# A two-layer hybrid block on one core: block sums and low parts by adding DMA, and three modulation sums moved

## The chip, the cores and the metric

The kernel runs on one core of a Trainium2 chip. The metric is the device time of one execution in microseconds, as the median of several runs.

## The reference, cut to what matters

A diffusion transformer of two layers works on 256 latent and 256 context tokens of width 1024, batch 1, in float32. Both streams are laid side by side, so that most products have 512 columns.

```python
for i in range(2):                       # layer 0: short convolution, layer 1: grouped attention
    mod  = silu(c)     @ mod_w[i] + mod_b[i]     # nine chunks of 1024 for the latent stream
    modc = silu(c_ctx) @ mod_w[i] + mod_b[i]     # the same for the context stream
    lat += 0.5 * mod[2] * swiglu(rms(lat) * g0 * (1 + mod[1]) + mod[0], w13[i, 0], w2[i, 0])
    cx  += 0.5 * modc[2] * swiglu(...same with modc...)
    h, hc = the two streams normed with chunks 3 and 4
    y, yc = conv(h), conv(hc)   or   attention(h, hc)
    lat += mod[5] * y           # and cx, while it is still read
    lat += 0.5 * mod[8] * swiglu(lat normed with chunks 6 and 7, w13[i, 1], w2[i, 1])
    # the same for cx in layer 0; in layer 1 the context ends with the attention

def swiglu(h, w13, w2):                  # 1024 -> 2 x 2816 -> 1024
    gate, up = split(h @ w13)
    return (silu(gate) * up) @ w2
```

## The kernel before, in words

**Arithmetic.** Every float32 matrix is split into a rounded high part and the rest, the low part, and a product is three matmuls: high by high, high by low, low by high (`mm3`, L136 to L138). `split` (L107, L108) makes the two parts: ScalarE copies the raw tile into the high part, VectorE subtracts it from the raw tile. `split_far` (L112 to L114) does without VectorE: ScalarE writes the high part and its negative, and a DMA issued by GpSimd reads the raw weights once more from memory and adds them onto the negative, which gives the low part.

**Weights.** `load_raw` (L103) brings up to 128 x 1024 float32 (512 KB) through SyncE's queue into a ring of eight buffers, `wr`. The high and low parts go into rings of four buffers, `wh` and `wl`, which TensorE frees when it has used them.

**First products.** The input products of the swiglus and of the convolution run over `Pair`s: two rows of output tiles of 128 at a time, with a seven-product scheme after Strassen and Winograd in place of eight, on blocks of 512 by 256. The scheme needs sums of weight blocks (S1 to S4) and of activation blocks (T1 to T4). A Pair loads two raw tiles r1 and r2 that hold its four weight blocks. For S1 GpSimd writes the negative of one block (L710), and an adding DMA of GpSimd puts another one onto it (L713). VectorE forms S2 in place (L732) and S3, S4 (L740); `keep` splits each pair of sums with one 1024-wide `split`. `head` computes the products with A11 and A12, `five` the one with S1, `six` those with S2 and S4, `seven` and `four` those with S3 and A22, which are taken one Pair later. A22's parts come from `split_far`. The first two input tiles of a stage go by plain products in `opening`, while the norm of the second stream is still being made; `opening` also sets up the first Pair, called head there.

**Second products.** The 22 rows of hidden tiles are taken in thirds of 8, 7 and 7. After each third `project` multiplies what there is by the matching part of w2, for eight output tiles m; `ws2` loads and splits the weights of one m, and `get` keeps three m ahead. The first three m run interleaved with the last Pair's `seven` and `four`. A tile that doesn't end the swiglu is scaled by the modulation gate on ScalarE (L564) and added to x by an adding DMA of GpSimd (L567). In the last third VectorE does it (L573), the sums of squares for the next norm are gathered (`square_add`, L262), and the last two tiles are taken one stream after the other, so that the norm of the first stream (`rms_sum`, `rms_all`, `Blocks.block`) can be made while TensorE works on the second.

**Modulation.** Each of the 128 rows that remain after the start (56 of layer 0, 72 of layer 1) is a job: a 512 KB load, and one VectorE sum per stream (`mod_unit`, L177, 1024 products each), 224 sums in all. `tick(n)` lets n of them run at its place in the program; `tick(ev)` follows the first five tiles of each second product, and some Pairs. `mod_ready` and `gate_of` run at once whatever is still missing of a chunk that is needed.

**Order.** The start is written out by hand. Behind it the scheduler of the framework orders each engine's instructions by their place in the program and by when it reckons them ready; `tc.issue_after(i)` keeps instructions of i's engine behind i.

Of the kernel before, what the change touches and what calls it, by code (L numbers as in the profile page):

```python
# [9 lines left out]
F32 = mybir.dt.float32  # L10
# [6 lines left out]
P = 128  # L17
# [31 lines left out]
def hybrid_kernel(ctx: ExitStack, tc: tile.TileContext, a: dict, out: bass.AP):  # L49
# [51 lines left out]
    def load_raw(src, n=1024):  # L101
        raw = wp.tile([P, 1024], F32, name=nm("wr"), tag="wr", bufs=8)
        nc.sync.dma_start(raw[:, :n], src)  # L103
        return raw
# [143 lines left out]
        return get  # L248


    accs = {}

    def square_add(k, c0, c1):

# [9 lines left out]
    def rms_sum(s):  # L264

        pq = psmall("ss")
        for i in range(2):
            c = s * S + i * P
            nc.tensor.matmul(
                pq[:, S + i : S + i + 1], accs["t"][:, c : c + P], ones[:, 0:1],  # L270
                start=True, stop=True,
            )
        rs = tp.tile([P, 2], F32, name=nm("rs"), tag="rs")
        nc.scalar.activation(
            out=rs, in_=pq[:, S : S + 2], func=AF.Sqrt, scale=1.0 / D, bias=eps_t
        )
        ri = tp.tile([P, 2], F32, name=nm("ri"), tag="ri")
        nc.vector.reciprocal(ri, rs)
        return pq, ri
# [93 lines left out]
    class Blocks:  # L373
# [33 lines left out]
        def sums(self, n):  # L407

            r = self.raw
            b11, b12, b21, b22 = r[0, 0], r[0, 1], r[1, 0], r[1, 1]  # L410
            tt = nc.vector.tensor_tensor

            def keep(key, src):
                hi, lo = self.t[key] = hot("th"), hot("tl")
                split(hi, lo, src)

            if n == 0:
                tt(out=b11, in0=b12, in1=b11, op=ALU.subtract)
                keep("T1", b11)
            elif n == 1:  # L420
                tt(out=b12, in0=b22, in1=b12, op=ALU.add)
                tt(out=b22, in0=b22, in1=b11, op=ALU.add)
                keep("T2", b22)
            else:
                tt(out=b21, in0=b21, in1=b22, op=ALU.subtract)
                keep("T3", b12)
                keep("T4", b21)

    class FirstBlocks(Blocks):
# [13 lines left out]
        def sums(self):  # L443
            r = self.raw
            tt = nc.vector.tensor_tensor
            for key in ("T1", "T2", "T3", "T4"):
                self.t[key] = hot("th"), hot("tl")

            def keep(key, q, src):
                hi, lo = self.t[key]  # L450
                c = slice(q * T2, q * T2 + T2)
                split(hi[:, c], lo[:, c], src)

            b = lambda hf, s, q: r[2 * hf + q, s]
            for q in range(2):
                tt(out=b(0, 0, q), in0=b(0, 1, q), in1=b(0, 0, q), op=ALU.subtract)
                keep("T1", q, b(0, 0, q))
            for q in range(2):
                tt(out=b(0, 1, q), in0=b(1, 1, q), in1=b(0, 1, q), op=ALU.add)
                tt(out=b(1, 1, q), in0=b(1, 1, q), in1=b(0, 0, q), op=ALU.add)  # L460
                keep("T2", q, b(1, 1, q))
            for q in range(2):
                tt(out=b(1, 0, q), in0=b(1, 0, q), in1=b(1, 1, q), op=ALU.subtract)
                keep("T3", q, b(0, 1, q))
            for q in range(2):
                keep("T4", q, b(1, 0, q))
# [122 lines left out]
    def project(ws, src, nk, gate, tail, tot, late, ev, between=()):  # L589

        def products(ps, w, ks, c0, c1, wide=True):
            ms = [src(k, c0, c1) for k in ks]
            if wide and len(ms[0]) == 3:
                return mm_wide(ps, [w(k) for k in ks], ms, ks[0] == 0, ks[-1] == nk - 1)
            for k, m in zip(ks, ms):  # L600
                mm3(ps[:, : c1 - c0], w(k), m[:2], k == 0, k == nk - 1)

        nf = 3 if between else 2
        ahead = {}

        def get(m):
            for i in range(m, min(m + 3, KT)):
                if i not in ahead:
                    ahead[i] = ws(i)
            return ahead[m]  # L610

        w2 = [get(m) for m in range(nf)]
        p2 = [psum("py") for _ in range(nf)]
        cut = nk - 2 if between else nk - 1
        for i in range(nf):
            products(p2[i], w2[i], range(cut), 0, tot)
            if i < len(between):
                between[i]()
        if between:
            for i in range(nf):  # L620
                products(p2[i], w2[i], (nk - 2,), 0, tot)
        for i in range(nf):
            products(p2[i], w2[i], (nk - 1,), 0, tot)
            finish(i, p2[i], 0, tot, gate, tail, len(src(0, 0, tot)) == 3)
            tick(ev)

        for m in range(nf, KT - late):
            if tail and tot == S and m == KT - 2:
                ready()
            w = get(m)  # L630
            ps = psum("py")
            wide = len(src(0, 0, tot)) == 3 and m < KT - 1
            products(ps, w, range(nk), 0, tot, wide)
            finish(m, ps, 0, tot, gate, tail, wide)
            if m < 5 - late:
                tick(ev)
            if late and tail and m == KT - late - 2:
                ready()
        if late:

            wl = [get(m) for m in (6, 7)]
            for s in range(2):
                for i in range(2):
                    ps = psum("py")
                    products(ps, wl[i], range(nk // 2), s * S, s * S + S)
                    flush(1)
                    products(ps, wl[i], range(nk // 2, nk), s * S, s * S + S)
                    finish(6 + i, ps, s * S, s * S + S, gate, tail)
# [48 lines left out]
    class Pair:  # L697
# [5 lines left out]

        def __init__(self, src, h):
            self.h, self.w, self.src = h, {}, src
            r2 = load_raw(src[:, 1024:2048])
            r1 = wp.tile([P, 1024], F32, name=nm("wr"), tag="wr", bufs=8)
            nc.sync.dma_start(r1[:, T2:], src[:, T2:1024])

            nc.gpsimd.tensor_scalar(  # L710
                out=r1[:, :T2], in0=r2[:, :T2], scalar1=-1.0, scalar2=None, op0=ALU.mult
            )
            nc.gpsimd.dma_start(out=r1[:, :T2], in_=src[:, :T2], accum_op=ALU.add)  # L713
            self.raw = [r1, r2]
            ts = half()
            for i, key in enumerate(("A11", "A12")):
                self.w[key] = [t[:, i * T2 : i * T2 + T2] for t in ts]
                split(*self.w[key], self.raw[i][:, T2:])

        def keep(self, keys, part):  # L720
            hi, lo = half()
# [4 lines left out]
        def sums(self, n):  # L726

            r1, r2 = self.raw
            s1, s2 = r1[:, :T2], r1[:, T2:]
            tt = nc.vector.tensor_tensor  # L730
            if n == 0:
                tt(out=s2, in0=s2, in1=s1, op=ALU.subtract)  # L732
                self.keep(("S1", "S2"), r1)
                return
            self.w["A22"] = [
                wp.tile([P, T2], F32R, name=nm(t), tag=t, bufs=2) for t in ("w4h", "w4l")
            ]
            split_far(*self.w["A22"], r2[:, :T2], self.src[:, 1024 : 1024 + T2])
            v = lambda t: t.rearrange("p (a c) -> p a c", a=2)
            tt(  # L740
                out=v(r2), in0=v(r2), in1=s2.unsqueeze(1).to_broadcast([P, 2, T2]),
                op=ALU.subtract,
            )
            self.keep(("S3", "S4"), r2)
# [44 lines left out]
    def opening(h, srcs, post):  # L789

        w = [load_w(srcs[0])]
        pp = [(psum("pg"), psum("pu")) for _ in range(2)]
        w13_mm(pp[0], w[0], h, range(KT), 0, S)
        flush(1)
        w.append(load_w(srcs[1]))
        at = w13_mm(pp[1], w[1], h, range(2), 0, S)
        with tc.issue_after(at):
            flush()
        with tc.issue_after(every[-1]):
            w13_mm(pp[1], w[1], h, range(2, KT), 0, S)  # L800
        h.sums(0)
        w13_mm(pp[0], w[0], h, range(KT), S, T2)
        post(pp[0], 0)
        head = srcs[2]()
        h.sums(1)
        head.sums(0)
        w13_mm(pp[1], w[1], h, range(KT), S, T2)
        post(pp[1], 1)
        head.head()
        head.sums(1)  # L810
        h.sums(2)
        return head

    def ffn(l, b, h, tot, gate, tail, gs=(), ev=(0, 0), z=None):
        gs = list(gs)
        i0 = 0
        for t, n in enumerate(THIRDS):
# [78 lines left out]
            def ws2(m):  # L896
# [1 line left out]
                o = (m % 2) * n * P  # L898
                raw = load_raw(src[:, o : o + n * P], n * P)
                hi, lo = half()  # L900
                split(hi[:, : n * P], lo[:, : n * P], raw[:, : n * P])
                return lambda k: (hi[:, k * P : k * P + P], lo[:, k * P : k * P + P])

            cur = gs
# [722 lines left out]
```

## Time and profile before

| | |
|---|---|
| median of 3 runs | 1545.36 us (1543.89 to 1546.64) |
| profiled execution | 1544.66 us |
| its span, first to last instruction | 1542.9 us |
| TensorE, matmuls | busy 1533.0 us, 99% |
| VectorE | busy 1296.8 us, 84% |
| ScalarE | busy 850.5 us, 55% |
| GpSimd | busy 299.3 us, 19% |
| moved by DMA | 278.80 MB, mean 181 GB/s |

The stages, by when TensorE starts on them in the trace: the first swiglu to 376 us (its second products from 110, 224 and 333), the convolution to 549 (its output product from 510), the second swiglu to 897, the third to 1245, then attention and, from 1353, the last swiglu on 256 columns. In the rows PE is TensorE's matmuls and PEld its weight loads, DVE is VectorE, ACT ScalarE, POOL GpSimd and SP SyncE; L with a number is a line of the kernel. A row of a timeline has start and length in us, engine, line, operation, the tile written and those read, and in brackets the engine's idle time before it with what ended it. A row of the groups has the count, the busy time in us, the mean in ns, and the idle time before.

### The profile page before, as it was taken

What the parts mean: (1) busy time and instruction counts of PE and PEld (TensorE: products, weight loads), DVE (VectorE), ACT (ScalarE), POOL (GpSimd) and SP (SyncE); (2) the same over time, 40 slices, a digit from 0 to 9 for tenths busy, and PEclk for the clock granted to TensorE, in tenths of its full rate; (3) what the DMA queues carried; (4) which work ended last, traced back from release to release, by engine and by line L of the source; (5) the groups of instructions that cost most, each with busy time, mean ns of one, the idle gap of its engine ahead of it and who ended that gap; (6) DMA issues with size and microseconds to landing.
All of it is one profiled execution on the core that took longest, in us unless ns stands there. A gap on an engine that the chain in (4) does not pass through costs nothing.

```text
span 1542.9 us, 27460 instructions
## 1 busy us (share of the span) xinstructions
PE 1533.0 (99%) x10652; PEld 1424.7 (92%) x10652; DVE 1296.8 (84%) x1974; ACT 850.5 (55%) x1476; POOL 299.3 (19%) x265
## 2 busy tenths in 40 slices
PE   9999999999999999999999999999999999999999
PEld 7898998999999899989899899989999899998888
DVE  5889788898999999978979889958968788997676
ACT  5744554646665376446456476446456456774553
POOL 0003313402231012042142102142052002300000
PEclk9999999999999999999999999999999999999999
DMA  9568768775366645686796635786697743476562
GB/s 367 211 191 236 159 185 227 172 196 142 75 144 183 197 104 143 216 209 147 213 210 150 212 74 126 222 186 145 209 222 177 257 156 113 147 246 220 170 195 75
DMA packets 97474, 278.80 MB, mean 181 GB/s; under 512 B 11456, under 2 KB 13120, under 8 KB 97344
## 3 DMA queue, kind: packets, MB, share of 16 engines
q1 hardware_dynamic: 69408, 228.10, 45.8%
q0 software_dynamic: 25920, 47.20, 18.1%
q10 hardware_dynamic: 2016, 1.76, 0.4%
q8 instruction: 83, 1.36, 0.4%
q14 instruction: 47, 0.39, 0.1%
HBM read 262.07 MB, written 1.05 MB: 171 GB/s over the span
## 4 chain that ended last, share of the span: by engine, by line
PE 90%; DVE 5%; DMA 2%; issue 1%; ACT 1%; POOL 0%; SPq 0%; DVEq 0%; ACTq 0%; POOLq 0%
PE py L137 8%; PE py L136 8%; PE py L138 8%; PE p L138 8%; PE p L136 8%; PE p L137 8%; PE q L138 6%; PE q L136 6%; PE q L137 6%; PE py L144 2%; PE pu L144 2%; PE pg L144 2%; DMA wr<-in_w 2%; DVE wl L108 1%; PE py L146 1%
## 5 line engine op out<-in xcount | busy, mean ns | idle before, releaser
L107 ACT ACTIVATE wh<-wr 128x1024 fp32r<-128x1024 f32 (+2 forms) x454 | 401.3, 909 | 291.0 <-PE py L137 98.6
L108 DVE TENSOR_TENSOR wl<-wr,wh 128x1024 fp32r<-128x1024 f32 (+2 forms) x454 | 467.0, 1052 | 106.3 <-ACT wh L107 87.6
L177 DVE CUSTOM_DVE_ANT_0 junk<-wr,scbc,first 128x1024 bf16<-128x1024 f32 x209 | 271.0, 1296 | 2.3 <-DMA wr<-in_modT 0.3
L137 PE MATMUL py<-gl,wh 128*128 128x512 f32 (+1 forms) x570 | 213.4, 374 | 0.0
L136 PE MATMUL py<-gh,wh 128*128 128x512 f32 (+1 forms) x570 | 213.4, 374 | 0.0
L138 PE MATMUL py<-gh,wl 128*128 128x512 f32 (+1 forms) x570 | 212.8, 373 | 0.0
L710 POOL TENSOR_SCALAR wr<-wr 128x512 f32<-128x512 f32 x66 | 123.5, 1871 | 423.8 <-DMA wr<-in_w 223.0
L136 PE MATMUL p<-th,wh 128*128 128x256 f32 x528 | 149.5, 283 | 0.1
L138 PE MATMUL p<-th,wl 128*128 128x256 f32 x528 | 149.4, 283 | 0.0
L137 PE MATMUL p<-tl,wh 128*128 128x256 f32 x528 | 149.4, 283 | 0.0
L138 PEld LDWEIGHTS py<-gh,wl 128*128 128x128 f32 x570 | 107.3, 188 | 19.2
L136 PEld LDWEIGHTS py<-gh,wh 128*128 128x128 f32 x570 | 107.4, 188 | 18.3
L137 PEld LDWEIGHTS py<-gl,wh 128*128 128x128 f32 x570 | 107.4, 188 | 18.1
L138 PE MATMUL q<-bh,wl 128*128 128x256 f32 x400 | 113.2, 283 | 0.0
L136 PE MATMUL q<-bh,wh 128*128 128x256 f32 x400 | 113.2, 283 | 0.0
L137 PE MATMUL q<-bl,wh 128*128 128x256 f32 x400 | 113.2, 283 | 0.0
L136 PEld LDWEIGHTS p<-th,wh 128*128 128x128 f32 x528 | 101.3, 192 | 0.7 <-ACT sg L757 0.3
L137 PEld LDWEIGHTS p<-tl,wh 128*128 128x128 f32 x528 | 101.3, 192 | 0.4
L138 PEld LDWEIGHTS p<-th,wl 128*128 128x128 f32 x528 | 101.3, 192 | 0.0
L114 POOL DMA_DIRECT2D w4l<-in_w x56 | 53.5, 955 | 229.1 <-ACT w4l L113 182.7
L567 POOL DMA_DIRECT2D x<-yg x48 | 44.2, 985 | 212.6 <-ACT yg L564 180.5
L740 DVE TENSOR_TENSOR wr<-wr,wr 128x1024 f32<-128x1024 f32 x66 | 81.2, 1230 | 2.0 <-issue 0.3
(323 smaller groups left out, 4159.1 us busy)
## 6 DMA issues: line engine op xcount, KB each, us to landing
wr<-in_w SPq DMA_DIRECT2D x120, 512.0 KB, 4.8
wr<-in_modT SPq DMA_DIRECT2D x113, 512.0 KB, 4.9
wr<-in_w2b SPq DMA_DIRECT2D x64, 448.0 KB, 4.0
wr<-in_w2a SPq DMA_DIRECT2D x32, 512.0 KB, 4.6
wr<-in_w SPq DMA_DIRECT2D x56, 256.0 KB, 4.3
wr<-in_w POOLq DMA_DIRECT2D x56, 256.0 KB, 6.1
w4l<-in_w POOLq DMA_DIRECT2D x56, 256.0 KB, 6.1
x<-yg POOLq DMA_DIRECT2D x48, 256.0 KB, 7.3
```

What stands on the lines that cost most here:

```text
L107: nc.scalar.activation(out=hi, in_=src, func=AF.Copy)
L108: return nc.vector.tensor_tensor(out=lo, in0=src, in1=hi.bitcast(F32), op=ALU.subtract)
L114: nc.gpsimd.dma_start(out=lo, in_=src, accum_op=ALU.add)
L136: nc.tensor.matmul(ps, wh, mh, start=first, stop=False, **kw)
L137: nc.tensor.matmul(ps, wh, ml, start=False, stop=False, **kw)
L138: return nc.tensor.matmul(ps, wl, mh, start=False, stop=last, **kw).ins
L144: nc.tensor.matmul(ps, w[0], m[2], start=first and n == 0, stop=False)
L146: nc.tensor.matmul(ps[:, :S], w[1], m[0], start=False, stop=last and n == len(ms) - 1)
L177: nc.vector.tensor_tensor_reduce(out=junk, in0=raw, in1=scbc[:, v, :], scale=0.5 if ch in (2, 8) else 1.0, scalar=modb[:, l, col : col + 1 ...
L567: nc.gpsimd.dma_start(out=x[:, m, :], in_=t, accum_op=ALU.add)
L710: nc.gpsimd.tensor_scalar(out=r1[:, :T2], in0=r2[:, :T2], scalar1=-1.0, scalar2=None, op0=ALU.mult)
L740: tt(out=v(r2), in0=v(r2), in1=s2.unsqueeze(1).to_broadcast([P, 2, T2]), op=ALU.subtract,)
```

## The change

Four things are changed.

1. A Pair's first load takes blocks 1 and 2 of its four in one 512 KB transfer, and the adding DMA puts block 0 onto block 2, which gives S1 as a sum instead of a difference. GpSimd's negation and the separate 256 KB load go. The signs of the activation sums change with it (`Blocks.sums`, `FirstBlocks.sums`), and S1 and S2 change places in r1.
2. In the second products of the three swiglus with 512 columns, output tiles 2 and 3 of the first two thirds and output tile 2 of the last get their low part by `split_far` instead of `split`.
3. After output tile 5, the sixth, of a second product that doesn't end a swiglu, three more modulation sums are due, as long as more than 90 jobs remain.
4. The norm's root instructions are recorded, and in `opening` the ScalarE instructions of the head's `sums(1)` are kept behind the latest of them.

```diff
-    accs = {}
+    accs, roots = {}, []
...
-        nc.scalar.activation(
+        roots.append(nc.scalar.activation(
             out=rs, in_=pq[:, S : S + 2], func=AF.Sqrt, scale=1.0 / D, bias=eps_t
-        )
+        ).ins)
...
             elif n == 1:
-                tt(out=b12, in0=b22, in1=b12, op=ALU.add)
-                tt(out=b22, in0=b22, in1=b11, op=ALU.add)
+                tt(out=b12, in0=b22, in1=b12, op=ALU.subtract)
+                tt(out=b22, in0=b22, in1=b11, op=ALU.subtract)
...
             finish(m, ps, 0, tot, gate, tail, wide)
+            if m == 5 and not tail and len(jobs) > 90:
+                tick(3)
             if m < 5 - late:
                 tick(ev)
...
             self.h, self.w, self.src = h, {}, src
+            r1 = load_raw(src[:, T2 : T2 + 1024])
+            nc.gpsimd.dma_start(out=r1[:, T2:], in_=src[:, :T2], accum_op=ALU.add)
             r2 = load_raw(src[:, 1024:2048])
-            r1 = wp.tile([P, 1024], F32, name=nm("wr"), tag="wr", bufs=8)
-            nc.sync.dma_start(r1[:, T2:], src[:, T2:1024])
-
-            nc.gpsimd.tensor_scalar(
-                out=r1[:, :T2], in0=r2[:, :T2], scalar1=-1.0, scalar2=None, op0=ALU.mult
-            )
-            nc.gpsimd.dma_start(out=r1[:, :T2], in_=src[:, :T2], accum_op=ALU.add)
             self.raw = [r1, r2]
             ts = half()
             for i, key in enumerate(("A11", "A12")):
                 self.w[key] = [t[:, i * T2 : i * T2 + T2] for t in ts]
-                split(*self.w[key], self.raw[i][:, T2:])
+                split(*self.w[key], self.raw[i][:, i * T2 : i * T2 + T2])
...
-            s1, s2 = r1[:, :T2], r1[:, T2:]
+            s1, s2 = r1[:, T2:], r1[:, :T2]
             tt = nc.vector.tensor_tensor
             if n == 0:
-                tt(out=s2, in0=s2, in1=s1, op=ALU.subtract)
-                self.keep(("S1", "S2"), r1)
+                tt(out=s2, in0=s1, in1=s2, op=ALU.subtract)
+                self.keep(("S2", "S1"), r1)
                 return
...
         head.head()
-        head.sums(1)
+        with tc.issue_after(roots[-1]):
+            head.sums(1)
         h.sums(2)
...
                 hi, lo = half()
-                split(hi[:, : n * P], lo[:, : n * P], raw[:, : n * P])
+                if tot == T2 and (m == 2 or m == 3 and t < 2):
+                    split_far(hi[:, : n * P], lo[:, : n * P], raw[:, : n * P], src[:, o : o + n * P])
+                else:
+                    split(hi[:, : n * P], lo[:, : n * P], raw[:, : n * P])
```

More of the change, by code (lines that the diff above doesn't have):

```diff
@@ L458, in sums @@
             for q in range(2):
-                tt(out=b(0, 1, q), in0=b(1, 1, q), in1=b(0, 1, q), op=ALU.add)
-                tt(out=b(1, 1, q), in0=b(1, 1, q), in1=b(0, 0, q), op=ALU.add)
+                tt(out=b(0, 1, q), in0=b(1, 1, q), in1=b(0, 1, q), op=ALU.subtract)
+                tt(out=b(1, 1, q), in0=b(1, 1, q), in1=b(0, 0, q), op=ALU.subtract)
                 keep("T2", q, b(1, 1, q))
```

## The prediction

> **What bounds the kernel now.** I read the page first, then the waits of TensorE's weight loads between 200 and 1245 us, which holds every stage that the change can reach after the start, then the timelines of single engines around the few waits found.
>
> ```profile
> PE 1533.0 (99%) x10652; PEld 1424.7 (92%) x10652; DVE 1296.8 (84%) x1974; ACT 850.5 (55%) x1476; POOL 299.3 (19%) x265
> ...
> PE 90%; DVE 5%; DMA 2%; issue 1%; ACT 1%; POOL 0%; SPq 0%; DVEq 0%; ACTq 0%; POOLq 0%
> ```
>
> TensorE is busy for 99% of the span and carries 90% of the chain. The change adds and removes no matmul. So it can win only what TensorE now loses in waits, and those are few:
>
> ```profile
> PEld pg L136 <- ACT bh L391: 2.1, 3, 1.6
> PEld p L138 <- DVE wl L108: 1.0, 2, 0.8
> PEld q L138 <- DVE wl L108: 0.6, 2, 0.3
> PEld pg L137 <- DVE bl L392: 0.6, 2, 0.4
> PEld p L136 <- ACT sg L757: 0.3, 1, 0.3
> ...
> ```
>
> The columns are total, times, longest, in us. These are 4.6 us in ten waits, and each is followed by about 0.1 us until the matmuls run at their pace again. So about 5.6 us, 0.36% of the time, is the ceiling of any gain here. All of them wait for VectorE or ScalarE, none directly for a transfer. There is no such ceiling on a loss.
>
> The largest, 1.6 us, is at the border from the convolution's output product to the second swiglu:
>
> ```profile
> 547.14 0.28 PE L137 MATMUL py<-zl,wh 128*128 128x256 f32 x1
> 547.26 0.28 PE L138 MATMUL py<-zh,wl 128*128 128x256 f32 x1
> 548.97 0.39 PE L136 MATMUL pg<-bh,wh 128*128 128x256 f32 x1 [1.43 <-ACT bh L391]
> ```
>
> Matmuls of this shape start 0.12 us apart; here the next starts 1.71 us later, so 1.59 us is lost. VectorE before it:
>
> ```profile
> 528.53 1.28 DVE L177 CUSTOM_DVE_ANT_0 junk<-wr,scbc,first 128x1024 bf16<-128x1024 f32 x1
> ...
> 542.16 1.27 DVE L177 CUSTOM_DVE_ANT_0 junk<-wr,scbc,first 128x1024 bf16<-128x1024 f32 x1
> ...
> 543.85 0.47 DVE L573 SCALAR_TENSOR_TENSOR x<-py,mod,x 128x256 f32<-128x256 f32 x1
> ...
> 546.91 1.26 DVE L299 SCALAR_TENSOR_TENSOR t<-x,A,ss 128x256 f32<-128x256 f32 x3
> ...
> 554.46 1.22 DVE L108 TENSOR_TENSOR wl<-wr,wh 128x1024 fp32r<-128x1024 f32 x1
> ```
>
> From 528.53 to 542.16 the timeline holds eight modulation sums (L177), of which the first and last are shown, and no gap. The eighth tile's first half leaves TensorE near 541 (counted back from 547.4: 48 matmuls of 0.12 us and some 0.7 us of the norm's own), but is added to x only at 543.85. The count of ticks explains the eight: the first swiglu gives 71 sums, the convolution's parts 5 and its output product 12, so 88 are done, while the next norm needs 96 (chunks 2 to 7 of layer 0). The trace's 89th to 96th sums are these.
>
> **The change part by part.** *Six sums moved.* The new tick comes at the sixth tile of the first two products of the first swiglu: jobs left are 128 at the start and about 98 there, over 90; in later stages they are fewer. So six sums run near 145 and 250 us instead of near 530 to 542, and two stay of the eight. Their loads move with them, three of 512 KB on SyncE's queue, in front of the next parts' weights. That takes 6 x 1.28 = 7.7 us out of VectorE's queue ahead of the wait. How long the norm takes on a free VectorE is seen at the border before:
>
> ```profile
> 369.86 0.48 DVE L573 SCALAR_TENSOR_TENSOR x<-py,mod,x 128x256 f32<-128x256 f32 x1 [0.63 <-PE py L138]
> ...
> 374.42 0.90 ACT L391 ACTIVATE bh<-t,mod 128x256 fp32r<-128x256 f32 x2
> ```
>
> From the addition to x to the first normed block it is 4.6 us. From 541 that gives 545.6, before TensorE has finished at 547.4, so the 1.6 us go, if ScalarE's order lets them:
>
> ```profile
> 547.46 1.06 ACT L107 ACTIVATE wh<-wr 128x1024 fp32r<-128x1024 f32 x1 [2.23 <-PE py L137]
> 548.42 0.89 ACT L391 ACTIVATE bh<-t,mod 128x256 fp32r<-128x256 f32 x2
> ```
>
> A weight's high part stands ahead of the block here and waits for a buffer that TensorE frees at its end. The scheduler put it there with the eight sums in its reckoning; with two it should put the block first, as at the border before. The small waits up to 557 (bl, 0.6 us, with two restarts 0.2) come from the same backlog, as the split at 554.46 between two blocks shows: 0.8 us more. Next behind would be the 0.2 us waits that the other borders keep. Sum of this part: -2.4 us.
>
> *Block sums by an adding DMA.* Each of 66 Pairs drops GpSimd's negation (L710). Its first load grows from 256 to 512 KB, and comes before the second instead of after it; the adding DMA stays. GpSimd loses about 121 us, which is on no path by itself. But VectorE is slowed beside it:
>
> ```profile
> L710 POOL TENSOR_SCALAR wr<-wr x66: 1482/1830/3444, 73.4 to 1174.9; 128x512 f32<-128x512 f32 x66
> ```
> ```profile
> L732 DVE TENSOR_TENSOR wr<-wr 128x512 f32<-128x512 f32 x66 | 45.7, 693 | 10.2 <-DMA wr<-in_w 10.0
> ```
> ```profile
> 428.07 1.11 DVE L732 TENSOR_TENSOR wr<-wr 128x512 f32<-128x512 f32 x1
> ...
> 428.04 1.48 POOL L710 TENSOR_SCALAR wr<-wr 128x512 f32<-128x512 f32 x1 [5.99 <-DVE wl L108]
> ```
> ```profile
> 926.19 2.77 DVE L108 TENSOR_TENSOR tl<-hr,th 128x1024 fp32r<-128x1024 f32 x2
> ...
> 926.68 2.08 POOL L710 TENSOR_SCALAR wr<-wr 128x512 f32<-128x512 f32 x1 [17.18 <-DMA wr<-in_w]
> ```
>
> The VectorE sum of 0.69 us took 1.11 us beside the negation at 428, and two splits of 1.22 us, overlapping by 0.09, took 2.77 instead of 2.35 at 926: 0.42 us each time, and one of the two engines gives way, since the negation itself stretches from 1.48 to as much as 3.44 us. Right behind these two spots stand the waits for wl at 432 (0.3) and 930 (0.2, and a trace more at 934). With their restarts they are 0.7 us, and 0.42 us earlier clears them. The 0.8 us wait for wl at 410 has no slowed VectorE row in front and stays. Sum: -0.7 us. [...]
>
> *Low parts by adding DMA.* In the three swiglus of 512 columns, tiles 2 and 3 of the first two second products and tile 2 of the third, 15 in all, leave VectorE. It saves 3 x (2 x 1.22 + 3 x 1.09) = 17.1 us (1.09 is the 896-wide split quoted below), in stages where TensorE waits for nothing, so nothing on the path. ScalarE gets a second copy each, about 1 us in a queue that is 55% busy. The question is when the low part lands:
>
> ```profile
> DMA to landing us min/median/max: 3.9/5.9/9.0
> ```
> ```profile
> DMA to landing us min/median/max: 4.2/7.3/10.8
> ```
> ```profile
> q1 hardware_dynamic: 69408, 228.10, 45.8%
> q0 software_dynamic: 25920, 47.20, 18.1%
> ```
> ```profile
> 750.66 0.95 ACT L107 ACTIVATE wh<-wr 128x896 fp32r<-128x896 f32 x1 [2.36 <-PE p L137]
> ...
> 762.95 0.39 PE L136 MATMUL py<-gh,wh 128*128 128x512 f32 x1
> ```
>
> The first landing row is of the block sums' adds (L713), the second of the adds to x (L567), both 256 KB. The queues' shares give 0.181 x 1542.9 / 47.2 = 5.9 us of all 16 engines per added MB, so 448 KB instead of 256 KB costs 1.2 us more: 7.1 to 8.5 us typically, 12.0 at worst. The fourth tile's high part ends at 751.6, its negative copy would at 752.6, and TensorE starts that tile at 762.95: 10.3 us. So the cover is 2 to 3 us typically and minus 1.7 at worst. The third tile and the other products stand alike. I take a few short waits, +0.2 us, nearer to the medians; the ends are 0 and the first rival. The added traffic, 66 x 256 KB plain and 7.3 MB adding, costs 3.5% + 2.8% of the engines' time by the same two rows, which lifts a share of about 65% to 71%.
>
> *The head's last sums behind the root.* At the three openings the first Pair's A22 copies move on ScalarE behind the second norm root. Their consumers are four products later; queued behind them are only the second half's blocks, and the 2.4 us in which ScalarE waits for that norm cover the 1.3 us. Nothing. The changed signs cost nothing either: same instructions.
>
> *The third part's first Pair.* Here the change gives and takes:
>
> ```profile
> 250.00:275.00 25.00, 24.81 (x146) 21.87 (x145) 18.60 (x23) 13.65 (x25) 12.85 (x12) 1.00 0.97 236
> ```
> ```profile
> 256.69 0.92 POOL L713 DMA_DIRECT2D wr<-in_w  x1 [0.41 <-POOL wr L710]
> ```
> ```profile
> 252.65 1.09 DVE L108 TENSOR_TENSOR wl<-wr,wh 128x896 fp32r<-128x896 f32 x1 [3.13 <-ACT wh L107]
> ...
> 262.66 0.69 DVE L732 TENSOR_TENSOR wr<-wr 128x512 f32<-128x512 f32 x1 [1.72 <-DMA wr<-in_w]
> 263.27 1.28 DVE L177 CUSTOM_DVE_ANT_0 junk<-wr,scbc,first 128x1024 bf16<-128x1024 f32 x1
> ...
> 266.81 2.36 DVE L108 TENSOR_TENSOR wl<-wr,wh 128x1024 fp32r<-128x1024 f32 x2
> ```
>
> VectorE waits for the add that lands at 262.66, and its first low part ends at 268.0, where TensorE waits 0.3 us for wl and then 0.3 for sg, 0.7 with restarts. Without the negation the add can start some 1.8 us earlier and needs one load instead of two. Against that stand three more sums (3.8 us) and up to two more loads of 512 KB where the DMA engines are 97% busy (0.5 MB at 236 GB/s is 2.2 us each). VectorE's holes of 3.1 and 1.7 us, and the two splits taken away before them, cover the sums if those run before 262. The ends are -0.7 and +3.8; I take -0.3, since the sum's chain is shortened by as much as one load costs.
>
> **Sum.** -2.4 - 0.7 + 0.2 - 0.3 = -3.2 us. Made against the profiled execution (1542.9 us of span, 1544.66 us with what lies around it) that is 1541.5; the execution stands 0.7 us under the median of 1545.36, so for the median it is 1542.2.
>
> **The rivals.**
>
> *The adds land late (slower).* The price is paid at the third or fourth tile of nine second products. It decides when the adds of 448 and 512 KB land on average later than 10.3 us after issue; at 10.65 us the loss, 9 x 0.35, eats the gain. If they took 7.3 us in proportion to bytes (12.8) it would be 9 x 2.5 = 22 us; at 11.2 us it is 9 x 0.9 - 3.2 = +5, so 1550. For it: the worst add to x took 10.8 us, and these stretches load modulation rows too. Against it: the medians, and GpSimd is idle there. [...]
>
> *The three sums fall in front of the first Pair's low part.* All 3.8 us are paid at 268: -3.2 + 0.3 + 3.8, so 1546.3. For it: two sums already stand between 263 and 267.
>
> *ScalarE's order stays.* The block stays behind the weight's high part at 547.46, and the 2.4 us do not come: 1544.6. The change would not do what it says there.
>
> **How the numbers follow.** A measurement of this kernel can tell about 0.2%, 3.1 us, from no change. Forecast 0.57 (1540.0 to 1543.8; of this 0.42 below 1542.3 and 0.15 above). Late adds 0.20 (0.18 slower, 0.02 within). Sums in front 0.10 (0.08 within, 0.02 slower). Order stays 0.13 (0.12 within, 0.01 faster). So faster 0.43, same 0.37, slower 0.20. The range from 1540.0 to 1549.5 leaves out the upper half of the late adds and the forecast's low tail.
>
> **What would show it.** Right: no wait of over 0.3 us before the first pg after 547; two sums, not eight, in the 15 us before that border; L710 gone as a negation; VectorE's total down by some 17 us for the splits and more for the meetings with GpSimd; the 256-wide waits near 432 and 930 gone. Wrong: waits of TensorE for a DMA into wl in the second products, a wait over 1 us in the first Pair after 264, or new waits at the openings, where the head's copies were moved.

## The result, and the profile after

| | before | after |
|---|---|---|
| median | 1545.4 us (1543.89 to 1548.86, 15 runs) | 1542.21 us (1540.89 to 1543.2, 15 runs) |
| ratio | | 0.9974, 95% interval 0.9967 to 0.9981 |
| profiled execution, span | 1544.66 us, 1542.9 us | 1543.2 us, 1541.4 us |

The change wins 3.2 us by the medians (4.0 by the ratio, whose interval is 2.9 to 5.1), where -3.2 and 1542.2 were forecast. A ratio compares the undisturbed runs of a kernel and of the kernel before on the same chip, so it is not exactly the quotient of the medians. The profiled execution of after is the longest of its 15 runs, which matters for the last swiglu below.

The page of after, busy time and DMA queues:

```profile
PE 1531.7 (99%) x10652; PEld 1423.5 (92%) x10652; DVE 1267.4 (82%) x1959; ACT 862.8 (56%) x1491; POOL 194.4 (13%) x214
...
q1 hardware_dynamic: 69408, 245.40, 48.7%
q0 software_dynamic: 28080, 54.47, 20.9%
...
```

VectorE is down by 29.4 us (1296.8 to 1267.4), of which the 15 splits are 17.1 by the prediction's estimate. GpSimd is down by 105, and the two queues take 69.6% of the DMA engines' span where they took 63.9 (45.8 + 18.1): 5.7 points more, 6.3 forecast. TensorE's waits between 200 and 1245 us in after (total, times, longest):

```profile
PEld p L138 <- DVE wl L108: 0.8, 1, 0.8
PEld ss L269 <- DVE acc L262: 0.8, 4, 0.2
PEld pg L136 <- ACT bh L391: 0.5, 2, 0.2
PEld q L138 <- DVE wl L108: 0.3, 1, 0.3
PEld p L136 <- ACT sg L754: 0.3, 1, 0.3
```

2.7 us are left of 4.8 (the 4.6 of the prediction's rows, and one wait of 0.2 us for the norm's sum in the row below them). The wait of 1.6 us for the block bh, those for bl, and two for wl are gone; the 0.8 us at 410 stays, and the norm's sum, `ss`, now waits four times instead of once, 0.2 us at most. Where the time was won is read from one instruction, the norm's first sum, in both traces (before, after at its first and last place; then before and after at the border to the third swiglu):

```profile
L269 PE MATMUL ss<-ones,acc x36: 164/250/271, 371.3 to 1357.0; 128*128 128x1 f32 x36
```
```profile
L269 PE MATMUL ss<-ones,acc x36: 164/250/271, 371.4 to 1354.3; 128*128 128x1 f32 x36
```
```profile
892.61 0.27 PE L269 MATMUL ss<-ones,acc 128*128 128x1 f32 x1
```
```profile
890.17 0.27 PE L269 MATMUL ss<-ones,acc 128*128 128x1 f32 x1
```

At 371 after is 0.1 us late, at 892 it is 2.4 early, at 1357 2.7; at the end only 1.5 (1542.9 to 1541.4). So 2.5 us came between 371 and 892, 0.3 behind it, and 1.2 was lost again in the last swiglu. At the border behind the convolution, after:

```profile
533.31 1.28 DVE L177 CUSTOM_DVE_ANT_0 junk<-wr,scbc,first 128x1024 bf16<-128x1024 f32 x1
...
540.61 0.48 DVE L573 SCALAR_TENSOR_TENSOR x<-py,mod,x 128x256 f32<-128x256 f32 x1 [1.43 <-PE py L138]
```
```profile
544.54 0.51 ACT L391 ACTIVATE bh<-t,mod 128x256 fp32r<-128x256 f32 x1 [1.52 <-DVE t L299]
544.96 1.04 ACT L107 ACTIVATE wh<-wr 128x1024 fp32r<-128x1024 f32 x1
```
```profile
547.30 0.28 PE L138 MATMUL py<-zh,wl 128*128 128x256 f32 x1
547.42 0.28 PE L136 MATMUL pg<-bh,wh 128*128 128x256 f32 x1
```

From 528 to the border VectorE runs three modulation sums where there were eight, at 528.19, 530.21 and, shown, 533.31. The norm's scale is computed from its chunks at 532.02, so the first two are the ones that were still due, and the third is not for this norm. VectorE now waits for TensorE before the last addition to x, at 540.61 instead of 543.85. The first block stands ahead of the weight's high part on ScalarE, at 544.54 instead of 548.42. TensorE's step at the border is 0.12 us, as inside a product.

### The profile page after: what moved, and what is told of

Read it like the earlier page. It is cut to its first block, busy times and chain, and to the rows that moved or that the text cites. A ratio compares the mean times of both kernels' runs of the same rounds, so it can differ in the third digit from the quotient of the medians.

```text
span 1541.4 us, 27350 instructions
## 1 busy us (share of the span) xinstructions
PE 1531.7 (99%) x10652; PEld 1423.5 (92%) x10652; DVE 1267.4 (82%) x1959; ACT 862.8 (56%) x1491; POOL 194.4 (13%) x214
## 4 chain that ended last, share of the span: by engine, by line
PE 91%; DVE 4%; DMA 3%; issue 1%; ACT 1%; SPq 0%; POOL 0%; DVEq 0%; ACTq 0%; POOLq 0%
PE py L137 8%; PE py L136 8%; PE py L138 8%; PE p L138 8%; PE p L136 8%; PE p L137 8%; PE q L138 6%; PE q L136 6%; PE q L137 6%; PE py L144 2%; PE pu L144 2%; PE pg L144 2%; DMA wr<-in_w 2%; DVE junk L177 1%; PE pg L136 1%; PE pg L138 1%
## 5 line engine op out<-in xcount | busy, mean ns | idle before, releaser
L108 DVE TENSOR_TENSOR wl<-wr,wh 128x1024 fp32r<-128x1024 f32 (+2 forms) x439 | 443.8, 1033 | 127.5 <-ACT wh L107 108.8
L107 ACT ACTIVATE wh<-wr 128x1024 fp32r<-128x1024 f32 (+2 forms) x439 | 386.4, 907 | 266.0 <-PE py L137 97.9
L177 DVE CUSTOM_DVE_ANT_0 junk<-wr,scbc,first 128x1024 bf16<-128x1024 f32 x209 | 267.4, 1280 | 3.0 <-DMA wr<-in_modT 0.8
L709 POOL DMA_DIRECT2D wr<-in_w x56 | 49.2, 878 | 446.7 <-DMA wr<-in_w 250.4
L573 DVE SCALAR_TENSOR_TENSOR x<-py,mod,x 128x256 f32<-128x256 f32 x117 | 52.8, 478 | 35.7 <-PE py L138 24.7
```

The source lines that it names most:

```text
L107: nc.scalar.activation(out=hi, in_=src, func=AF.Copy)
L108: return nc.vector.tensor_tensor(out=lo, in0=src, in1=hi.bitcast(F32), op=ALU.subtract)
L177: nc.vector.tensor_tensor_reduce(out=junk, in0=raw, in1=scbc[:, v, :], scale=0.5 if ch in (2, 8) else 1.0, scalar=modb[:, l, col : col + 1 ...
L573: nc.vector.scalar_tensor_tensor(out=x[:, m, s * S : s * S + S], in0=ps[:, o : o + S], scalar=g[:, m, s : s + 1], in1=x[:, m, s * S : s * ...
L709: nc.gpsimd.dma_start(out=r1[:, T2:], in_=src[:, :T2], accum_op=ALU.add)
```

## The experiments

All ratios are to the kernel before, with 95% intervals; the changed kernel's is 0.9974.

### One part alone

**ticks_only**: the kernel before and only part 3, three more sums at each of two places.

```diff
             finish(m, ps, 0, tot, gate, tail, wide)
+            if m == 5 and not tail and len(jobs) > 90:
+                tick(3)
```

> The kernel before with the three sums at the sixth tile alone. By the prediction's sum the 1.6 us wait at the border behind the convolution goes, with some 0.8 us of small ones behind it, and the three sums in the first swiglu's second product are no longer helped by the missing negation: the waits of the third part's first Pair (0.6 us before) grow to 1 to 3 us. So 0 to 2.4 us faster, most likely 1.5. The rival, that relief of VectorE anywhere clears the border, says that the sums moved do no more for it than their share of the relief: about 0.5 us.

**sums_only**: only the block sums by the adding DMA (part 1 of the change).

> The kernel before with the block sums by an adding DMA alone, without the order behind the root. By the prediction's sum the waits for wl near 432 and 930 us go, the waits of the third part's first Pair shrink, the wait at the border stays at 1.6 us: 0.7 to 1.4 us faster. The rival, that relief of VectorE anywhere clears the border, expects 1.5 to 2.5 us faster, with the border's wait gone or halved.

**lows_only**: only the low parts by `split_far` (part 2).

> The kernel before with the fifteen low parts by an adding DMA alone. By the prediction's sum VectorE is 17 us less busy and nothing is gained: 0.5 us faster to 0.5 us slower, no wait of TensorE for these low parts, or a few under 0.5 us. Late adds as a theory expect waits for a DMA into wl and 1 to 5 us slower. The rival of relief anywhere expects 1 us faster.

**no_ticks**: the changed kernel without those two lines of part 3.

> The changed kernel without the three sums at the sixth tile. By the prediction's sum 2.4 us of the gain are lost, and the third part's first Pair has no wait left: about 0.8 to 1.4 us faster than before, with the border's wait of 1.6 us back. The rival of relief anywhere expects most of the gain kept: 2 to 3 us faster than before.

| kernel | median us | ratio |
|---|---|---|
| ticks_only | 1551.02 | 1.0047 (1.0034 to 1.0059) |
| sums_only | 1546.94 | 1.0014 (1.0005 to 1.0023) |
| lows_only | 1544.36 | 0.9996 (0.9987 to 1.0005) |
| no_ticks | 1543.2 | 0.9988 (0.9979 to 0.9997) |

Two parts lose alone, one does nothing, and together with the fourth they win: the terms cannot be added as the prediction added them. Part 4 alone was not run. The largest waits of ticks_only, of sums_only and of no_ticks, 200 to 1245 us:

```profile
PEld p L136 <- ACT sg L759: 4.2, 1, 4.2
PEld ss L269 <- DVE acc L262: 2.4, 1, 2.4
```
```profile
PEld ss L269 <- DVE acc L262: 3.1, 3, 2.2
PEld pg L136 <- ACT bh L391: 2.1, 3, 1.6
```
```profile
PEld pg L136 <- ACT bh L391: 2.1, 3, 1.6
```

no_ticks has the wait for bh back at 1.6 us, and ticks_only has lost it: the moved sums alone turn the order at that border. But in ticks_only two other waits take its place, 4.2 us in the third part's first Pair (the place of the second rival) and 2.4 us for the norm's sum at 552. sums_only has the second kind too. The next runs take these two apart.

### The norm's wait: the head's copies and the root

**no_root**: the changed kernel without part 4.

```diff
-        with tc.issue_after(roots[-1]):
-            head.sums(1)
+        head.sums(1)
```

> The changed kernel without one of its parts: the head's last sums are no longer held behind the second norm root at the three openings; all else stays. Theory (order): in the run with the block sums alone, ScalarE's copy of the head's A22 stood ahead of the root, waited for its load, and TensorE lost 2.2 us at 894 and 0.6 at 372 in the norm's wait; holding the sums behind the root is what averts this here. Then those two waits come back, 1.5 to 5 us in all: 1544 to 1547 us. Rival (the prediction's price for this part, nothing): 1542.2, with no wait of the norm over 0.3 us.

**ticks_root**: the kernel before with parts 3 and 4.

> The kernel before plus two parts of the change: the three sums at the sixth tile, and the head's last sums held behind the second norm root. Theory: the sums alone lost 5.1 us at 269 to 275 (no room) and 2.3 us at 552 (the head's copy ahead of the root); the root order takes away the second alone, so +6.0 becomes +3.7: 1548.5 to 1549. Rival 1: holding the copies back shifts the head's transfers to a worse place and a wait of over 1 us stands at an opening all the same: 1550 or more. Rival 2: the loss at 269 to 275 hung on the same order, so that both go and the 2 us at 549 to 557 are gained: 1543.

no_root took 1547.81 us, ratio 1.0016 (1.0007 to 1.0024): the part priced at nothing holds the whole gain and more. ScalarE of no_root, and the two larger of TensorE's three waits for the norm's sum (the third is 0.6 us at 372):

```profile
543.74 0.63 ACT L112 ACTIVATE w4h<-wr 128x512 fp32r<-128x512 f32 x1 [4.29 <-DMA wr<-in_w]
...
544.94 0.40 ACT L260 ACTIVATE sq<-x 128x256 f32<-128x256 f32 x1
```
```profile
545.85 0.38 PE L269 MATMUL ss<-ones,acc 128*128 128x1 f32 x2 [2.58 <-DVE acc L262]
```
```profile
896.66 0.27 PE L269 MATMUL ss<-ones,acc 128*128 128x1 f32 x1 [1.80 <-DVE acc L262]
```

ScalarE stands 4.29 us at the head's A22 copy, whose raw tile has not landed. The last square of the norm, whose input is ready at 541.9, is queued behind it and runs at 544.94. In the kernel before, the copy stood one square earlier and cost nothing, because its tile, the first of the two loads, had landed at 538.4:

```profile
538.39 0.63 ACT L112 ACTIVATE w4h<-wr 128x512 fp32r<-128x512 f32 x1 [0.89 <-DMA wr<-in_w]
...
539.59 0.40 ACT L260 ACTIVATE sq<-x 128x256 f32<-128x256 f32 x1
```

The block sums by an adding DMA make that tile, r2, the second load, and at two borders that alone puts the copy in the norm's way: sums_only waits 0.7 us at 372 and 2.2 at 894. At the border behind the convolution sums_only has no such wait, and ticks_only, where r2 is still the first load, has one of 2.4 us. There ScalarE stands 3.51 us at a copy of the same kind, by the order of the loads that of the Pair after the head, with two squares behind it:

```profile
548.93 0.63 ACT L112 ACTIVATE w4h<-wr 128x512 fp32r<-128x512 f32 x1 [3.51 <-DMA wr<-in_w]
...
550.13 0.40 ACT L260 ACTIVATE sq<-x 128x256 f32<-128x256 f32 x1
```

So both parts bring such waits, and part 4 averts them; by which path the moved sums bring theirs is not shown. ticks_root took 1550.48 us, ratio 1.0036 (1.0023 to 1.0048), with no wait of the norm over 0.2 us and a span 2.1 us shorter than ticks_only's (1549.7 and 1551.8); the 4.2 us at 276 stay. So the order averts the norm's wait there too, and not the other. The time is 1.5 us over the 1548.5 to 1549 expected. One wait of TensorE for a weight's high part near 269, 0.2 us in ticks_only, is 0.8 here; the rest of the miss stays open. The clock is no reason for it: behind the 4.2 us it is 0.50 in both traces, and the 6.0 us from which the expectation started were measured with it (ticks_root; the columns are explained with lows_from_1 below, 0.50 is TensorE's granted clock):

```profile
276.30:280.30 4.00, 4.00 (x20) 4.00 (x20) 3.86 (x7) 1.24 (x2) 2.62 (x3) 0.50 0.86 295
```

The intervals of ticks_only and ticks_root overlap, so this step rests on their waits.

### Room for the sums in the third part's first Pair

**no_lows**: the changed kernel with all low parts on VectorE.

```diff
-                if tot == T2 and (m == 2 or m == 3 and t < 2):
-                    split_far(hi[:, : n * P], lo[:, : n * P], raw[:, : n * P], src[:, o : o + n * P])
-                else:
-                    split(hi[:, : n * P], lo[:, : n * P], raw[:, : n * P])
+                split(hi[:, : n * P], lo[:, : n * P], raw[:, : n * P])
```

> The changed kernel with the low parts of the second products on VectorE again; block sums, root order and the three sums at the sixth tile stay. Theory (room): the 15 splits taken from VectorE are what makes room for the three added sums ahead of the third part's first Pair; without it TensorE waits there, 4 to 5 us as in the run with the sums alone (4.1 + 0.9 near 270 to 275): 1546 to 1548. Rival 1: dropping the negation made the room, then the wait near 268 stays under 1 us and the time is 1542 to 1543. Rival 2: the low parts only remove waits of their own, as alone (0.6 us): 1542.8 to 1543.2.

It took 1544.59 us, ratio 0.9996 (0.9987 to 1.0004): 2.4 us of the gain are gone by the medians (3.4 by the ratios), between the theory and the first rival. VectorE's first sum of the Pair (S2) in ticks_only, no_lows and after:

```profile
266.69 0.69 DVE L734 TENSOR_TENSOR wr<-wr 128x512 f32<-128x512 f32 x1 [3.33 <-DMA wr<-in_w]
```
```profile
263.01 0.69 DVE L729 TENSOR_TENSOR wr<-wr 128x512 f32<-128x512 f32 x1 [1.77 <-DMA wr<-in_w]
```
```profile
262.74 0.69 DVE L729 TENSOR_TENSOR wr<-wr 128x512 f32<-128x512 f32 x1 [0.99 <-DMA wr<-in_w]
```

The new block sums bring it from 266.69 to 263.01 (no_lows has the root order too, but that alone left the 4.2 us in ticks_root). no_lows still waits in and behind this Pair:

```profile
PEld p L136 <- DVE p L774: 1.4, 1, 1.4
PEld q L138 <- DVE wl L108: 1.0, 2, 0.8
```

The 0.8 us lie at 268 in this Pair, and a small one at 276. The 1.4 us lie at 283, where the first Pair's last product waits for a VectorE row that is queued behind a later Pair's S2, and this S2 stands for its adding DMA:

```profile
282.22 0.69 DVE L729 TENSOR_TENSOR wr<-wr 128x512 f32<-128x512 f32 x1 [1.55 <-DMA wr<-in_w]
```

In after this row waits 0.53 us, and only the two waits of 0.3 us near 268 and 270 are left. So both parts count here, and most of the room is the block sums'. The 1.4 us are a late transfer, not a want of room on VectorE; how the low parts bring that about is not shown.

### VectorE beside GpSimd

**idle_negation**: the changed kernel with a negation per Pair whose result nobody reads.

```diff
             r2 = load_raw(src[:, 1024:2048])
+            nc.gpsimd.tensor_scalar(
+                out=tp.tile([P, T2], F32, name=nm("ng"), tag="ng", bufs=1), in0=r2[:, :T2],
+                scalar1=-1.0, scalar2=None, op0=ALU.mult,
+            )
```

> The changed kernel plus, for each Pair, a GpSimd negation of 128x512 elements into a tile that nobody reads; it delays no transfer of its own Pair. Theory (contention, the prediction's step): VectorE rows beside it become longer by about 0.4 us, and the waits for wl near 432 and 930 come back, 0.2 to 0.3 us each: +0.7, so 1542.9. Rival 1: the negation mattered through its place in front of the adding transfer, so nothing comes back without that: 1542.2. [...]

It took 1544.97 us, ratio 0.9997 (0.9988 to 1.0006), 0.23%, 2.8 us by the medians, above the changed kernel, where the theory had 0.7 us. Its page and its waits:

```profile
PE 1532.5 (99%) x10652; PEld 1424.6 (92%) x10652; DVE 1282.4 (83%) x1959; ACT 862.5 (56%) x1491; POOL 305.2 (20%) x280
```
```profile
PEld q L138 <- DVE wl L108: 2.2, 3, 1.0
PEld ss L269 <- DVE acc L262: 1.4, 4, 0.8
...
PEld py L138 <- DMA wl<-in_w2b: 0.7, 1, 0.7
```

With the same 1959 instructions VectorE is busy 15.0 us longer, 0.23 us for each of 66 negations. The waits near 433 (0.67 us lost by the starts of the matmuls) and 934 (0.37) come back as the theory said. At three more places TensorE loses more than in after: 0.68 us at 268, 0.63 at 544 and 0.45 at 763. At 433 and 544 a VectorE row is stretched beside a negation. At 433 it is the split at 431.40, which takes 1.63 us here and 1.22 in after, with a negation beside it from 430.97 to 432.83. At 544 it is one that takes 0.43 us in after (VectorE, GpSimd):

```profile
542.95 1.06 DVE L262 TENSOR_TENSOR acc<-acc,sq 128x256 f32<-128x256 f32 x1 [0.54 <-ACT sq L260]
```
```profile
542.95 1.65 POOL L712 TENSOR_SCALAR ng<-wr 128x512 f32<-128x512 f32 x1
```

The wait at 763, the last of those above, is for an adding DMA. No negation runs from 745 to 770, and lows_only and six_late each have a wait of 0.2 us of this kind near 1210. So contention is shown at 433 and 544; at 268 and 934 the time lost came with the negations too, but no row here shows what was stretched, and 763 is not shown to be such a place.

### How much cover the adds have

**lows_from_1**: the second output tile of all nine second products too.

```diff
-                if tot == T2 and (m == 2 or m == 3 and t < 2):
+                if tot == T2 and (m in (1, 2) or m == 3 and t < 2):
```

> The changed kernel with the low parts of the second tile of all nine second products by adding transfers too (24 instead of 15). In the changed kernel these transfers land 7.9 to 10.1 us after issue, median 8.9, and TensorE waits for none of them. The second tile starts some 7 us after its negative copy could end. Theory (cover decides): each of the nine waits about 1.9 us, 17 in all at most, and some less where the load comes early: 1550 to 1559. Rival: the scheduler's early loads cover these as well, and VectorE's 10 us more of room change nothing: 1542.2.

It took 1566.37 us, ratio 1.0132 (1.0116 to 1.0148): 24 us over the changed kernel, more than the 17 at most. Landing of these adds in after and here, and who waits here:

```profile
DMA to landing us min/median/max: 7.9/8.9/10.1
```
```profile
  PEld py L138: 20.8, 9
  PE py L138: 16.9, 9
...
DMA to landing us min/median/max: 8.2/9.8/12.2
```

The matmuls idle 16.9 us in nine waits, as the theory had it. The rest is the clock. Stretches of this trace (length; busy us of PE, PEld, DVE, ACT, POOL; then PEclk, the granted clock, DMA share, GB/s):

```profile
118.40:120.40 2.00, 2.00 (x8) 1.62 (x9) 1.96 (x4) 0.00 (x0) 0.82 (x1) 0.88 1.03 272
120.40:123.60 3.20, 3.20 (x10) 2.48 (x9) 2.67 (x6) 0.00 (x0) 0.00 (x0) 0.54 1.06 349
...
235.40:238.00 2.60, 2.60 (x11) 2.15 (x12) 2.53 (x5) 0.00 (x0) 0.87 (x1) 1.00 1.03 300
```
```profile
645.20:648.80 3.60, 3.60 (x10) 2.78 (x11) 3.49 (x7) 0.00 (x0) 0.71 (x1) 0.55 1.03 304
...
1115.20:1119.50 4.30, 4.30 (x13) 3.38 (x14) 3.00 (x6) 0.00 (x0) 0.03 (x1) 0.66 1.06 318
```
```profile
1229.20:1232.80 3.60, 3.60 (x10) 2.78 (x11) 1.29 (x2) 0.00 (x0) 0.00 (x0) 0.53 1.02 358
```

Behind four of the nine waits the clock is 0.53 to 0.66 for 3.2 to 4.3 us. Length times the missing share gives 0.2 + 1.5, 1.6, 1.5 and 1.7, together 6.5 us; with 16.9 and nine restarts of 0.1 that is 24.3.

### Versions that could beat both

**six_first**: all six moved sums in the first part. **late_tick**: one sum of the last swiglu a step later. **six_late**: both.

```diff
-            if m == 5 and not tail and len(jobs) > 90:
-                tick(3)
+            if m == 5 and not tail and len(jobs) > 105:
+                tick(6)
```
```diff
-                        tick(1)
+                        tick(0 if i == 2 else 1)
...
-                    tick(1)
+                    tick(2 if i0 + i == EARLY else 1)
```

> The changed kernel with all six sums at the sixth tile of the first part and none at that of the second. Theory: the sums of the second part are what still makes TensorE wait twice near 268 to 270 (0.3 us each); moved to the first part these waits go and nothing else changes: 1541.6. Rival: six sums in a row are 7.7 us of VectorE where three are 3.8, and six loads of 512 KB stand in front of the first part's weights, so that TensorE waits near 130 to 160 us, 1 to 4 us: 1543 to 1546.

> The changed kernel with one modulation sum of the last swiglu moved from the third early block to the first later block. In the profile of the changed kernel VectorE stands 1.9 us at 1368.5 waiting for that sum's row, and TensorE loses 1.2 us at 1370 to 1374 behind it; the kernel before lost nothing there. Theory (VectorE's queue stands at the sum, which came early relative to its load because the stage starts earlier): these waits go: 1541.0. Rival: the waits at 1370 are those of the profiled execution alone, which was the longest of its runs, so the median stays at 1542.2.

> Both edits of the two runs before it on the changed kernel: six sums in the first part, and the last swiglu's sum later. If both theories hold, 1.8 us under the changed kernel: 1540.4. If the first part has no room for six sums, 1542 to 1545 with the waits near 130 to 160 us; if the last swiglu's waits were of one execution, 1541.6.

They took 1541.27 us, ratio 0.9981 (0.9972 to 0.9990), 1541.53, 0.9981 (0.9972 to 0.9990), and 1541.09, 0.9978 (0.9969 to 0.9987). None is told apart from the changed kernel. What late_tick moves is this row of after's VectorE, which stands 1.89 us for a modulation row, with TensorE's waits behind it between 1360 and 1400 us:

```profile
1368.54 1.28 DVE L177 CUSTOM_DVE_ANT_0 junk<-wm,scbc,first 128x1024 bf16<-128x1024 f32 x1 [1.89 <-DMA wm<-in_modT]
```
```profile
PEld pg L144 <- DVE hx L310: 1.0, 3, 0.6
PEld pg L138 <- DVE wl L108: 0.8, 1, 0.8
```

late_tick's trace has no wait in that stretch, and its span is 1539.3 us. But with the sum in its old place the waits of this stretch are 1.8 us in after, 2.0 in no_ticks, 0.4 in no_lows and in the kernel before, and none in idle_negation: they come and go, and whether the change makes them likelier stays open. The two 0.3 us at 268 come and go as well: late_tick's instructions there are the changed kernel's, and its trace has no wait at that place. Six sums in the first part brought no wait, so it has room for them.

## Why the prediction was right, point by point

- **The ceiling.** Right: no run went under what the waits allowed, and what the change won came out of the ten waits listed.
- **Six sums moved, -2.4.** Right in place and mechanism: two of the eight due sums are left at the border, the block is first on ScalarE, the step is 0.12 us. no_ticks brings the 1.6 us back; its time alone (0.9988 against 0.9974) would show it only just, as the intervals touch. The stretch from 371 to 892 won 2.5 us in the trace; forecast for it were this -2.4 and the half of -0.7 that lies at 432.
- **Block sums, -0.7.** The waits near 432, 930 and 934 went, as forecast, and the trace's gains (2.5 us to 892, 0.3 behind it) leave room for no more than that. The mechanism, VectorE slowed beside GpSimd, is shown by idle_negation. Its 0.23% is what 66 negations cost in the changed kernel, where they meet other rows; it is not the size of this term. Alone the part loses 0.1% (sums_only), by the norm's wait. One reading in this step was too simple: at 926 both engines give way, VectorE's splits by 0.42 us and the negation, which takes 2.08 us where the shortest takes 1.48.
- **Low parts, +0.2.** No wait came in the profile of after, and one of 0.2 us each in those of lows_only and six_late, so the size was right. The adds of 448 and 512 KB land at 8.9 us in the median and 10.1 at worst, against 7.1 to 8.5 and 12.0 estimated for 448 KB, with 10.3 us of cover. The rival of late adds was a close one: 1.4 us more at the median would have cost the nine tiles their cover, and lows_from_1 paid its full price one tile earlier.
- **Root order, "nothing".** This step was wrong, and the right total hides it. That its own cost is nothing holds; but it was priced against the queues of the kernel before, and two other parts change them: part 1 makes r2 the second load, and the moved sums bring a copy ahead of the squares behind the convolution. Without part 4 the change is slower (1.0016), and TensorE waits 5.4 us for the norm's sums. The row was there to see: ScalarE's 0.89 us wait for w4h at 538.39, in front of the norm's square.
- **The first Pair, -0.3.** The profile of after has +0.1 (two waits of 0.3 us, slightly longer than before), another trace of the same instructions (late_tick) has none, -0.7 with the restarts. The price of 3.8 us for the sums in front was real: ticks_only lost 5 us there (its waits of 4.2 and 1.0), and the block sums, with the low parts' help, took that away.
- **The sum.** It met the median, with the parts tied to each other instead of added: parts 1 and 3 alone lose 0.1% and 0.5%. The 1.2 us of the last swiglu in the profiled execution were not foreseen.

## What to carry to other kernels

Price a part of a change against the kernel that the other parts make, not against the one before: a load that becomes the second of two can block an engine's queue in which it used to be early, and sums moved elsewhere can put another load's copy there. Where an engine takes its instructions in order, as ScalarE did in no_root (the square was ready at 541.9 and ran at 544.94, behind the copy), ask of each one that waits for a load what stands behind it; a copy nobody needs yet stood in front of the norm that everybody waited for. And a wait can cost more than its own length: behind four of the nine waits of lows_from_1 the lower clock took another 1.5 to 1.7 us each.

## What the runs showed of the hardware

**Behind a wait of about 2 us TensorE's clock was lower for 3 us and more, but not each time.** By the idle time before a matmul and the granted clock behind it: 1.43 us at 548.97 in the kernel before, 1.00; 1.80 us at 896.66 in no_root, 0.72; 2.00 us at 894.37 in sums_only, 1.00; 2.58 us at 545.85 in no_root, 0.59; 3.99 us at 275.24 in ticks_only, 0.50. So near 2 us it went either way (no_root, then sums_only):

```profile
896.80:899.80 3.00, 3.00 (x19) 2.94 (x20) 1.10 (x4) 0.78 (x2) 0.00 (x0) 0.72 0.26 48
899.80:903.00 3.20, 3.20 (x22) 3.20 (x22) 2.84 (x8) 3.20 (x8) 0.00 (x0) 0.73 0.00 0
```
```profile
894.60:898.00 3.40, 3.40 (x30) 3.35 (x30) 1.82 (x5) 1.75 (x4) 0.00 (x0) 1.00 0.19 35
```

Why two waits of nearly one length had different ends, no run here shows.

**GpSimd's negations cost VectorE a little, on average.** 66 negations of 1.48 to 2.54 us took 15.0 us from VectorE (1282.4 us busy in idle_negation, 1267.4 in after), 0.23 us each. A VectorE row that starts first is stretched in some meetings and not in others: in the kernel before, a modulation sum that started at 1001.95, 0.05 us before a negation, took 2.09 us instead of 1.28, and a split that started at 592.07, 0.03 us before one, took 1.22 us as it does alone. Why, no run here shows.
